# Two 1024-column projections by seven half-size products for eight, with their results kept in DRAM until they are used

## The chip, the cores and the metric

The kernel runs on one core of one Trainium2 chip. The metric is the time of one execution in microseconds of device time. Three runs of the kernel before gave 1104.89, 1106.11 and 1106.81 us.

## The reference

One decoder layer on 512 tokens of width 2048, in float32. Cut to what matters here:

```
h    = rmsnorm(x, norm_in)                       # 512 x 2048
proj = h @ w_in                                  # one projection, split by columns into
# q_a (1024), k_cmp v_cmp k_slc v_slc k_win v_win (256 each), gate_a (48), z_a (1024),
# q_h f_h i_h z_h (1024 each)
o_a  = nsa_mixer(q_a, k_cmp, ..., gate_a, ...)   # 16 query heads, 4 KV heads:
                                                 # compressed + selected + window attention
o_h  = hgrn2_mixer(q_h, f_h, i_h, lb)            # 8 heads, i_h is the values
o_a  = head_rmsnorm(o_a) * silu(z_a)
o_h  = head_rmsnorm(o_h) * silu(z_h)
x    = rmsnorm(x + concat(o_a, o_h) @ w_out)
```

In `compress_blocks`, blocks of 32 tokens of k_cmp (and v_cmp) go through two small matrices, `w1` and `w2`.

## The kernel before

Every large product of the kernel has a left factor and a right factor that are each split into a high part (rounded to the matmul's type) and a low part (the rest). Three matmuls make one product: high by high, low by high, high by low. `load_w` (L276 to L283) loads a tile of 128x1024 weights by one DMA of 512 KB on SP's queue, ACT casts it to the high part (L281), and DVE subtracts to get the low part (L282). The activations h stand transposed in SBUF as 16 tiles of 128 features by 512 tokens, high (`hh`) and low (`hl`), and stay there.

A projection comes in two forms. `proj_fm` (L323 to L325) puts features on the partitions: per 128 columns it takes 16 feature tiles times 3 = 48 matmuls of 128x512. `proj_tm` (L348 to L350) puts tokens on the partitions: for 512 columns it takes 16 feature tiles times 4 token tiles times 3 = 192 matmuls of 128x512. The program's order on PE, ACT and DVE is made by `run`, which takes turns between two streams of work in proportion to numbers written beside them. All DMAs but a few stand on SP's queue, in program order.

The stages are, in order: `first_proj` (k_cmp's columns, while x and the first weights arrive); the reciprocal norm of each token (`x_norm`: a chain of small DVE instructions that ends in L210 and L211, then transposes on PE, L214) ; `blocks`, which scales k_cmp (L367), copies it within SBUF into overlapping blocks by eight DMAs (L369 to L372, two tiles of four) and adds the position vectors (L383); v_cmp's projection alone; v_slc's projection beside the compression of k (`compress`, w1 loads at L390); v_win's projection with gate_a and then k_slc/k_win's first pairs (`make_kd(0, 0)`, `make_kd(0, 1)`) and q's first pair (`make_q(0)`), beside the compression of v; the attention with the other q and k projections between its steps; `hgrn_v(0)`, the first half of i_h, alone (192 matmuls); the eight heads of HGRN2, two at a time, each pair beside a length of other projections given by FILL = (62, 62.5, 62, 41): among them `hgrn_v(1)`, the second half of i_h, and both halves of z_a; the gates beside z_h; and the output projection. The attention's masks are made by GpSimd at the start.

Two results of `proj_tm` stay in SBUF: i_h as tiles of the pool `late` (13 buffers) and z_a as tiles of the pool `slab` (25 buffers).

Of the kernel before, what the change touches and what calls it, by code (L numbers as in the profile page):

```python
# [17 lines left out]
P = 128  # L18
# [14 lines left out]
NLATE = 13  # L33
PJ = 4
AHEAD = 2
FILL = (62, 62.5, 62, 41)
# [8 lines left out]
def hymba_layer(ctx: ExitStack, tc: tile.TileContext, x, norm_in, w_in, pe_k, w1_k, w2_k,  # L45
# [9 lines left out]
    slab = ctx.enter_context(tc.tile_pool(name="slab", bufs=NSLAB))  # L55
# [8 lines left out]

    def sl(dt=FP32):
        return slab.tile([P, 512], dt, name=nm("s"), tag="s")

    space = {}
# [7 lines left out]
    def b4(tag, bufs, dt=FP32):  # L76
        return big.tile([P, WCOLS], dt, name=nm(tag), tag=tag, bufs=bufs)
# [65 lines left out]
    def load_raw(src, k0, kt, c0, c, eng=None):  # L143
        raw = b4("w", WBUF)[:, 0:kt * c].rearrange("p (k c) -> p k c", k=kt)
        (eng or nc.sync).dma_start(out=raw, in_=src[k0 * P:(k0 + kt) * P, c0:c0 + c].rearrange("(k p) c -> p k c", p=P))
        return raw
# [4 lines left out]
    for k0, kt in FIRST:  # L151
        cs = slice(k0 * P, (k0 + kt) * P)
        first_w.append(load_raw(w_in2, k0, kt, C_KC, 256))
        if kt == 2:
            w = b4("w", WBUF).rearrange("p (t c) -> p t c", t=NT)
            nc.sync.dma_start(out=w, in_=x2[:, cs].rearrange("(t p) c -> p t c", p=P))
            xt.append([w[:, t, :] for t in range(NT)])
        else:
            xt.append([sl() for _ in range(NT)])
            for t in range(NT):  # L160
                nc.sync.dma_start(out=xt[-1][t], in_=x2[t * P:(t + 1) * P, cs])
# [58 lines left out]
    def consts():  # L220
# [28 lines left out]
    nc.gpsimd.affine_select(out=maskc, in_=maskc, pattern=[[P, NT], [-16, 32]], compare_op=ALU.is_ge,
                            fill=BIG, base=-31, channel_multiplier=1)  # L250
    keepc = const.tile([P, NT, 32], FP32, name="keepc")
    nc.gpsimd.memset(keepc, 1.0)
    nc.gpsimd.affine_select(out=keepc, in_=keepc, pattern=[[P, NT], [-16, 32]], compare_op=ALU.is_ge,
                            fill=0.0, base=-31, channel_multiplier=1)
    hmf = [sl(), sl()]
    hmask = const.tile([P, 8, 128], I32, name="hmask")
    for m in hmf:
        nc.gpsimd.memset(m, 1.0)

    def window(v, h, step, lo, width):  # L260
        nc.gpsimd.affine_select(out=v, in_=v, pattern=[[0, 2], [-step, P // step], [0, h]], compare_op=ALU.is_ge,
                                fill=0.0, base=-lo, channel_multiplier=1)
        nc.gpsimd.affine_select(out=v, in_=v, pattern=[[0, 2], [step, P // step], [0, h]], compare_op=ALU.is_ge,
                                fill=0.0, base=lo + width - 1, channel_multiplier=-1)


    for mi, (h, step, lo, width) in enumerate([(1, 2, 0, 1), (2, 4, 0, 2), (4, 8, 2, 2), (4, 8, 0, 2),
                                               (8, 16, 0, 8), (16, 32, 8, 8), (16, 32, 0, 8)]):
        v = hmf[mi // 4][:, (mi % 4) * P:(mi % 4 + 1) * P]
        window(v.rearrange("p (j b h) -> p j b h", j=2, h=h), h, step, lo, width)  # L270
    for i in range(2):
        nc.gpsimd.tensor_copy(hmask[:, 4 * i:4 * i + 4, :].rearrange("p a b -> p (a b)"), hmf[i])


    def load_w(src, k0, kt, c0, c, wt=None, raw=None):
        if raw is None:  # L276
            raw = load_raw(src, k0, kt, c0, c)
        if wt is None:
            wt = (b4("w", WBUF, F32R), b4("w", WBUF, F32R))
        hi, lo = [w[:, 0:kt * c].rearrange("p (k c) -> p k c", k=kt) for w in wt]  # L280
        nc.scalar.copy(hi, raw)  # L281
        nc.vector.tensor_tensor(lo, raw, hi.bitcast(FP32), ALU.subtract)  # L282
        return hi, lo  # L283

    def first_proj(acc):
# [3 lines left out]
        def prepare(c):  # L289
            w = load_w(w_in2, FIRST[c][0], FIRST[c][1], C_KC, 256, raw=first_w[c])  # L290
            x_turn(c)
            return w

        w = prepare(0)
        for c, (k0, kt) in enumerate(FIRST):
            hi, lo = w
            for j in range(2):
                js = slice(j * P, (j + 1) * P)
                for k in range(kt):
                    kk = k0 + k  # L300
# [739 lines left out]
```

## Time and profile before

| | us |
|---|---|
| median of three runs (range) | 1106.11 (1104.89 to 1106.81) |
| the profiled execution, whole | 1106.74 |
| its span in the trace | 1104.7 |
| PE busy in the span | 1086.3 |
| DVE busy | 572.0 |
| ACT busy | 394.3 |
| GpSimd busy | 76.1 |

The span is the time from the first to the last record of the core's engines and DMA queues. The granted TensorE clock had a mean of 0.997 of full speed over the span. Busy time of DVE, ACT and GpSimd lies beside PE's wherever the order of the program lets it.

### The profile page before, as it was taken

The numbers are of one execution on the slowest core, as the hardware profiler recorded it, in microseconds if no ns is written. First come the engines' busy times: TensorE is split into PE (matmuls) and PEld (weight loads), VectorE is DVE, ScalarE is ACT, GpSimd is POOL, SyncE is SP. The second block draws the span as 40 slices with busy tenths as digits, with TensorE's granted clock in tenths as the row PEclk, the third lists the DMA queues.
The fourth block names the chain that finished last, engine by engine and source line by source line (L and its number), as shares of the span: only waits on it lengthen the run. The fifth ranks groups of instructions, "written<-read, shape, count | busy, mean of one in ns | idle before, by whom it ended". The sixth has DMA issues, their size and how long they took to land.

```text
span 1104.7 us, 15078 instructions
## 1 busy us (share of the span) xinstructions
PE 1086.3 (98%) x5682; PEld 896.8 (81%) x5682; DVE 572.0 (52%) x1438; ACT 394.3 (36%) x798; POOL 76.1 (7%) x134
## 2 busy tenths in 40 slices
PE   7999999999999999999999999999999999999996
PEld 6899987777677777888888888888888888888886
DVE  4614336666655746416645547546677536324332
ACT  6412326645345644223222222223333423324221
POOL 5000020110200200000000000000000000202010
PEclk9999999999999999999999999999999999999998
DMA  7446454232422211323222322222242333335223
GB/s 256 122 142 191 115 145 104 71 83 58 115 59 57 76 39 39 96 77 96 77 77 61 92 78 80 82 81 73 76 130 81 95 115 115 126 112 173 96 86 124
DMA packets 91751, 109.60 MB, mean 99 GB/s; under 512 B 5584, under 2 KB 60448, under 8 KB 91680
## 3 DMA queue, kind: packets, MB, share of 16 engines
q1 hardware_dynamic: 91680, 108.65, 34.0%
q8 instruction: 45, 0.74, 0.3%
q14 instruction: 26, 0.21, 0.1%
HBM read 93.95 MB, written 4.19 MB: 89 GB/s over the span
## 4 chain that ended last, share of the span: by engine, by line
PE 94%; DMA 2%; ACT 1%; DVE 1%; issue 1%; SPq 0%; ACTq 0%
PE pj L348 13%; PE pj L349 13%; PE pj L350 13%; PE pj L323 10%; PE pj L325 10%; PE pj L324 10%; PE ot L581 4%; PE pj L562 3%; PE lp L730 3%; DMA w<-in_w_in_dram 2%; PE lp L548 2%; PE lp L549 1%; PE pj L973 1%; PE pj L972 1%; PE pj L974 1%; PE lp L399 1%
## 5 line engine op out<-in xcount | busy, mean ns | idle before, releaser
L282 DVE TENSOR_TENSOR w<-w,w 128x1024 fp32r<-128x1024 f32 (+3 forms) x151 | 182.3, 1208 | 255.7 <-PE pj L349 87.1
L281 ACT CAST w<-w 128x1024 fp32r<-128x1024 f32 (+3 forms) x151 | 156.8, 1039 | 300.1 <-DMA w<-in_w_in_dram 188.7
L348 PE MATMUL pj<-w,hh 128*128 128x512 f32 (+2 forms) x608 | 229.1, 377 | 0.0
L349 PE MATMUL pj<-w,hl 128*128 128x512 f32 (+2 forms) x608 | 225.1, 370 | 0.0
L350 PE MATMUL pj<-w,hh 128*128 128x512 f32 (+2 forms) x608 | 224.5, 370 | 0.0
L323 PE MATMUL pj<-hh,w 128*128 128x512 f32 x480 | 194.8, 406 | 0.0
L325 PE MATMUL pj<-hh,w 128*128 128x512 f32 x480 | 189.1, 394 | 0.0
L324 PE MATMUL pj<-hl,w 128*128 128x512 f32 x480 | 188.9, 393 | 0.0
L350 PEld LDWEIGHTS pj<-w,hh 128*128 128x128 f32 x608 | 114.2, 188 | 18.8
L348 PEld LDWEIGHTS pj<-w,hh 128*128 128x128 f32 x608 | 114.5, 188 | 18.1 <-ACT s L486 0.4
L349 PEld LDWEIGHTS pj<-w,hl 128*128 128x128 f32 x608 | 114.5, 188 | 17.7
L325 PEld LDWEIGHTS pj<-hh,w 128*128 128x128 f32 x480 | 90.2, 188 | 19.4 <-issue 0.9
L324 PEld LDWEIGHTS pj<-hl,w 128*128 128x128 f32 x480 | 90.4, 188 | 16.9 <-issue 0.5
L323 PEld LDWEIGHTS pj<-hh,w 128*128 128x128 f32 x480 | 90.3, 188 | 16.9 <-issue 0.7
L522 ACT ACTIVATE s<-s,mn 128x128 f32<-128x128 f32 (+3 forms) x128 | 71.7, 561 | 41.6 <-DVE mn L517 36.5
L517 DVE CUSTOM_DVE_ANT_0 s<-s,lp 128x128 f32<-128x128 f32 (+3 forms) x128 | 60.3, 483 | 37.2 <-PE lp L549 18.5
L562 PE MATMUL pj<-ident,s 128*128 128x128 f32 x320 | 53.7, 275 | 0.7 <-ACT s L522 0.5
L581 PE MATMUL ot<-pt,s 128*64 128x512 f32 (+3 forms) x256 | 47.9, 441 | 1.4 <-ACT pt L571 1.4
L562 PEld LDWEIGHTS pj<-ident,s 128*128 128x128 f32 x320 | 39.5, 140 | 11.1 <-ACT s L522 4.7
L571 ACT COPY pt<-pj 128x256 f32<-128x256 f32 (+2 forms) x56 | 25.8, 461 | 48.0 <-PE pj L562 47.8
L581 PEld LDWEIGHTS ot<-pt,s 128*64 128x64 f32 x256 | 22.2, 136 | 23.5 <-issue 10.5
L348 PE MATMUL pj<-w,s 128*128 128x512 f32 x96 | 37.5, 391 | 0.0
(252 smaller groups left out, 1350.8 us busy)
## 6 DMA issues: line engine op xcount, KB each, us to landing
w<-in_w_in_dram SPq DMA_DIRECT2D x115, 512.0 KB, 3.6
w<-in_w_out_dram SPq DMA_DIRECT2D x32, 512.0 KB, 3.8
s<-s SPq DMA_DIRECT2D x56, 128.0 KB, 2.3
s<-in_x_dram SPq DMA_DIRECT2D x16, 256.0 KB, 6.5
l<-in_x_dram SPq DMA_DIRECT2D x12, 256.0 KB, 3.2
out_dram<-l SPq DMA_DIRECT2D x12, 256.0 KB, 2.7
w<-in_w_in_dram SPq DMA_DIRECT2D x5, 456.0 KB, 4.6
w<-in_cmp_w_k_dram SPq DMA_DIRECT2D x4, 512.0 KB, 5.8
```

What stands on the lines that cost most here:

```text
L281: nc.scalar.copy(hi, raw)
L282: nc.vector.tensor_tensor(lo, raw, hi.bitcast(FP32), ALU.subtract)
L323: nc.tensor.matmul(acc[j], wh, hh, start=kk == 0, stop=False)
L324: nc.tensor.matmul(acc[j], wh, hl, start=False, stop=False)
L325: nc.tensor.matmul(acc[j], wl, hh, start=False, stop=kk == NK - 1)
L348: nc.tensor.matmul(o, ah, hi[:, k, :], start=kk == 0, stop=False)
L349: nc.tensor.matmul(o, al, hi[:, k, :], start=False, stop=False)
L350: nc.tensor.matmul(o, ah, lo[:, k, :], start=False, stop=kk == NK - 1)
L517: nc.vector.tensor_tensor_reduce(out=y, in0=e["bias"][:, 384 - i * P:512], in1=lp, scale=1.0, scalar=3e38, op0=ALU.add, op1=ALU.min, accum ...
L522: nc.scalar.activation(y, y, AF.Exp, bias=mn, scale=-1.0, accum_out=e["ls"][:, 2 * i + b:2 * i + b + 1])
L562: nc.tensor.transpose(tps[:, j * P:(j + 1) * P], y[:, j * P:(j + 1) * P], ident)
L581: nc.tensor.matmul(e["ot"][b * 64:(b + 1) * 64, j * P:512], v_tok[j][:, b * 256 + g * DH:b * 256 + (g + 1) * DH], e["pt"][:, b, j * 512:38 ...
```

## The change

- The four `proj_tm` of i_h and z_a (1024 columns each) are taken out of the places where they stood. In their place there are two calls of `seven`, one for i_h and one for z_a, one after the other, in a stage of their own ahead of the compression and the attention.
- `seven` multiplies 12 of the 16 feature tiles, in six pairs of tiles, by seven products of half the size in each direction in place of eight: the left halves are two halves of the tokens in two feature tiles of a pair, the right halves are two blocks of 512 columns. Seven times 36 = 252 matmuls of 128x512, and the last four feature tiles go as before, 96 matmuls: 348 for 1024 columns, where it was 384. Two calls make 696 for 768.
- For this the sums of the activations' quarters (S1 to S4, `sums_of`, six times) are made on DVE and split by ACT and DVE, beside the projections of v_cmp, v_slc and v_win. S3 is put over one quarter of h (`third_sums`), which goes to DRAM first and is read back (`block_21_back`) behind the seven products. The sums of the weights' blocks are made in `first`, `second` and `third` on DVE, and the products are added together by `after_first` to `after_all`, on DVE and ACT.
- Results go via DRAM: k_cmp and v_cmp (`keep`), v_slc and v_win (`vt_scr`), i_h (`v_scr`), z_a (`z_scr`). They are loaded again (`rows_back`, and `blocks`, whose eight DMAs now read DRAM) where they are used.
- The SBUF of the first part (pools `s2`, `s14`, `w` with 20 buffers, `e`) is given back (`first_part.close()`) before the slabs and the weight buffers of the rest are taken from it. The masks are made behind that, on GpSimd.
- The compression of k stands beside `make_kd(0, 0)` and `make_q(0)`, that of v beside `make_kd(0, 1)`. `late` has 18 buffers, FILL is (44, 42, 40, 24), and the gates of z_a's second half and of z_h's first half both stand beside the last projection.

The instructions on PE go from 5192 matmuls to 5120, no other change there in number. DVE gets 111 more instructions of 128x1024, 128x512 and 128x256, ACT 37 more of these sizes and 16 issues of DMAs, GpSimd 14 issues, and SP 38.

The diff, cut to its core:

```diff
-NLATE = 13
+NLATE = 18
-FILL = (62, 62.5, 62, 41)
+FILL = (44, 42, 40, 24)
+PAIRS = 6
...
+    def keep(acc):
+        fs = [dram(), dram()]
+        for j in range(2):
+            f = ev()
+            nc.vector.tensor_tensor(f, acc[j], rs_bc, ALU.mult)
+            nc.sync.dma_start(out=fs[j], in_=f)
+        return fs
     def blocks(acc, pcol):
         kv = []
         for j in range(2):
-            f = sl()
-            nc.vector.tensor_tensor(f, acc[j], rs_bc, ALU.mult)
+            f = acc[j]
             e, o = sl(), sl()
             nc.sync.dma_start(out=e[0:64, :], in_=f[0:64, :])
             nc.sync.dma_start(out=e[64:128, 0:511], in_=f[0:64, 1:512])
...
+        def first(jj):
+            b22, b12, b11 = load(1, jj, 1), load(0, jj, 1), load(0, jj, 0)
+            sub(b12, b12, b22)
+            t2[jj] = pair()
+            sub(t2[jj], b12, b11)
+            return parts(b11), parts(t2[jj]), parts(b12)
+        def second(jj):
+            b21, t4 = load(1, jj, 0), pair()
+            add(t4, t2[jj], b21)
+            return parts(t4), parts(b21)
...
+        return (group(first, (("A11", "1", True), ("S2", "6", True), ("S3", "7", True)), after_first) +
+                group(second, (("A22", "4", True), ("A12", "1", False)), lambda: None) + rest(0, "14", after_second) +
+                group(third, (("S1", "5", True), ("S4", "3", True)), after_third) + rest(1, "35", after_all))
...
-    kblk = blocks(KC, 32)
-    run((proj_fm(VC, C_VC, 256), 1))
-    run((proj_tm([], w_in2, hT, C_VS, 256, vs_done), 21), (compress(kblk, w1_k, w2_k, True), 10))
-    vblk = blocks(VC, 48)
-    run((chain(proj_tm([], w_in2, hT, C_VW, 304, vw_done), make_kd(0, 0), make_kd(0, 1), make_q(0)), 56),
-        (compress(vblk, w1_v, w2_v, False), 20))
+    kf = keep(KC)
+    run((chain(second_proj(VC), proj_tm([], w_in2, hT, C_VS, 256, vs_done), proj_tm([], w_in2, hT, C_VW, 304, vw_done)),
+         70), (all_sums(), 7))
+    third_sums()
+    in_turn(seven(C_IH, v_done) + seven(C_ZA, z_done(0)))
+    first_part.close()
...
+    block_21_back()
+    kblk = blocks(kf, 32)
+    masks()
...
+    run((chain(make_kd(0, 0), make_q(0)), 22), (compress(kblk, w1_k, w2_k, True), 10))
+    v_tok += rows_back(vt_scr, sl)
+    vblk = blocks(vf, 48)
+    run((chain(make_kd(0, 1)), 11), (compress(vblk, w1_v, w2_v, False), 10))
...
-    run((hgrn_v(0), 41))
+    hv[0] = rows_back(v_scr[0], late)
-    fill = chain(hgrn_qf(1), hgrn_v(1), hgrn_qf(2), hgrn_qf(3), z_proj(C_ZA, sz[0]), z_proj(C_ZA + 512, sz[1]))
+    fill = chain(hgrn_qf(1), hgrn_qf(2), hgrn_qf(3), z_proj(C_ZH, sz[2]))
...
-    run((fill, 41), (gate_chunk(0, o_nsa[0:4], 2, sz[0]), 10.5))
-    run((z_proj(C_ZH, sz[2]), 41), (gate_chunk(1, o_nsa[4:8], 2, sz[1]), 10.5))
-    run((z_proj(C_ZH + 512, sz[3]), 41), (gate_chunk(2, o_h[0:4], 1, sz[2]), 10.5))
+    sz[0] = rows_back(z_scr[0][0], sl)
+    run((fill, 15), (gate_chunk(0, o_nsa[0:4], 2, sz[0]), 10.5))
+    sz[1] = rows_back(z_scr[0][1], sl)
+    run((z_proj(C_ZH + 512, sz[3]), 41),
+        (chain(gate_chunk(1, o_nsa[4:8], 2, sz[1]), gate_chunk(2, o_h[0:4], 1, sz[2])), 21))
```

**First place: SP's queue ahead of `make_kd(0, 0)`.** In the kernel before, these are the loads of v_win's last weights and then of the first four tiles of `make_kd` (w<-in_w_in, 128x8x128):

```order
L145 DMA w_1150<-in_w_in_dram 128x3x304
L390 DMA w_1165<-in_cmp_w_v_dram 128x4x256
L145 DMA w_1202<-in_w_in_dram 128x3x304
L145 DMA w_1208<-in_w_in_dram 128x304
L145 DMA w_1304<-in_w_in_dram 128x8x128
L145 DMA w_1334<-in_w_in_dram 128x8x128
L145 DMA w_1383<-in_w_in_dram 128x8x128
L145 DMA w_1413<-in_w_in_dram 128x8x128
```

The loads of `make_kd` stood right behind other weights.

In the kernel after, SP's queue at the same load, with the last two weight tiles of `seven` (128x2x512) ahead of it; `d` is a tile in DRAM, `s` a slab:

```order
L160 DMA w_2213<-in_w_in_dram 128x2x512
L160 DMA w_2243<-in_w_in_dram 128x2x512
L607 DMA s_2362<-d_498 64x512
L608 DMA s_2362<-d_498 64x511
L609 DMA s_2363<-d_498 64x512
L610 DMA s_2363<-d_498 64x511
L607 DMA s_2368<-d_499 64x512
L608 DMA s_2368<-d_499 64x511
L609 DMA s_2369<-d_499 64x512
L610 DMA s_2369<-d_499 64x511
L160 DMA w_2440<-in_w_in_dram 128x8x128
L633 DMA s_2460<-in_cmp_w_k_dram 128x2x64 x2
```

Eight block loads of k_cmp now stand between the last weights of `seven` and the first weights of `make_kd(0, 0)`. The first of them (L607) writes a slab that lies where the first part's tiles lay, and its last wait is for PE: for the last matmul of `seven`. The next matmul on PE is the first of `make_kd(0, 0)`, with the weights of the L160 row.

**Second place: SP's queue ahead of the compression of v.** Before, its block loads stood between weights of v_win's projection:

```order
L145 DMA w_1098<-in_w_in_dram 128x3x304
L369 DMA s_948<-s_946 64x512
L370 DMA s_948<-s_946 64x511
L371 DMA s_949<-s_946 64x512
L372 DMA s_949<-s_946 64x511
L369 DMA s_956<-s_954 64x512
L370 DMA s_956<-s_954 64x511
L371 DMA s_957<-s_954 64x512
```

After, L687 are the copies of q's first pair, which wait for that projection's result, and L1072 the loads of v_slc's and v_win's results from DRAM:

```order
L160 DMA w_2758<-in_w_in_dram 128x8x128
L687 DMA s_2637<-s_2640 64x512
L687 DMA s_2637<-s_2641 64x512
L687 DMA s_2638<-s_2640 64x512
L687 DMA s_2638<-s_2641 64x512
L1072 DMA s_2649<-d_178 128x512
L1072 DMA s_2650<-d_179 128x512
L1072 DMA s_2651<-d_180 128x512
L1072 DMA s_2652<-d_181 128x512
L607 DMA s_2657<-d_672 64x512
L608 DMA s_2657<-d_672 64x511
L609 DMA s_2658<-d_672 64x512
```

The block loads of v_cmp moved behind four copies and four loads; behind `make_q(0)`, 48 matmuls of `make_kd(0, 1)` stand on PE, and then the first matmul of the compression of v, which needs these blocks.

**Third place: DVE in the chain of the reciprocal norm.** Before:

```order
L130 TENSOR_TENSOR rxt_481<-rxi_478 128x4
L131 TENSOR_TENSOR rxt_481<-rxt_481,rxa_476 128x4
L282 TENSOR_TENSOR w_547<-w_544,w_546 128x1024
L132 TENSOR_SCALAR rxt_481<-rxt_481 128x4
L133 TENSOR_TENSOR rxi_478<-rxi_478,rxt_481 128x4
L223 COPY col<-tp_462 128x64
L130 TENSOR_TENSOR rxt_481<-rxi_478 128x4
L226 TENSOR_TENSOR lbt<-col 128x8
L131 TENSOR_TENSOR rxt_481<-rxt_481,rxa_476 128x4
```

After, with the sums of the first two pairs (L362 adds the parts of h, L367 is one of the sums):

```order
L145 TENSOR_TENSOR rxt_477<-rxi_474 128x4
L146 TENSOR_TENSOR rxt_477<-rxt_477,rxa_472 128x4
L302 TENSOR_TENSOR w_511<-w_508,w_510 128x1024
L147 TENSOR_SCALAR rxt_477<-rxt_477 128x4
L362 TENSOR_TENSOR w_538<-hh_15_135,hl_16_136 128x1024
L242 COPY col<-tp_458 128x64
L148 TENSOR_TENSOR rxi_474<-rxi_474,rxt_477 128x4
L367 TENSOR_TENSOR w_538<-w_538 128x256
L245 TENSOR_TENSOR lbt<-col 128x8
```

A 128x1024 and a 128x256 instruction of the sums stand within the chain that PE's transposes and `keep` wait for.

## Rows read from the trace of the kernel before

**Rows 1.** The page: busy time of PE, and granted clock in 40 slices.

```profile
PE 1086.3 (98%) x5682; PEld 896.8 (81%) x5682; DVE 572.0 (52%) x1438; ACT 394.3 (36%) x798; POOL 76.1 (7%) x134
...
PEclk9999999999999999999999999999999999999998
```

**Rows 2.** Windows (us; busy of PE, PEld, DVE, ACT, POOL; clock, DMA share, GB/s).

```profile
0.00:25.00 25.00, 19.45 (x95) 16.26 (x96) 12.18 (x18) 16.11 (x37) 14.58 (x34) 1.00 0.84 275
...
475.00:500.00 25.00, 25.00 (x112) 20.72 (x111) 4.90 (x4) 6.87 (x8) 0.00 (x0) 1.00 0.30 82
```

**Rows 3.** Waits of PE: line, releaser, us in total, times, longest.

```profile
PE lp L192 <- DMA w<-in_x_dram: 3.0, 1, 3.0
...
PE ot L581 <- ACT pt L571: 1.4, 2, 0.8
...
PE tp L214 <- DVE rs L210: 0.2, 1, 0.2
```

**Rows 4.** Timeline of SP, the block copies (start, duration, line).

```profile
43.02 0.53 SPq L369 DMA_DIRECT2D s<-s  x1
43.60 0.58 SPq L370 DMA_DIRECT2D s<-s  x1
...
47.44 1.42 SPq L372 DMA_DIRECT2D s<-s  x1
```

**Rows 5.** DMA issues: KB each, median us to landing.

```profile
w<-in_w_in_dram SPq DMA_DIRECT2D x115, 512.0 KB, 3.6
...
s<-s SPq DMA_DIRECT2D x56, 128.0 KB, 2.3
```

**Rows 6.** The chain of waits that ended last: start, us, what.

```profile
254.31 4.21 DMA w<-in_w_in_dram
258.60 1.05 ACT w L281
```

**Rows 7.** Groups by line and shape: busy us, mean ns; idle before.

```profile
L282 DVE TENSOR_TENSOR w<-w,w 128x1024 fp32r<-128x1024 f32 x143 | 174.9, 1224 | 241.3 <-PE pj L349 85.7 <-ACT w L281 71.4 <-PE pj L324 54.7
...
L709 DVE TENSOR_TENSOR s<-s,s 128x256 f32<-128x256 f32 x56 | 23.9, 427 | 13.3 <-PE tp L775 9.3 <-POOL s L745 3.1 <-ACT s L759 0.2
...
L598 DVE TENSOR_TENSOR s<-tp,ls 128x512 f32<-128x512 f32 x16 | 11.0, 688 | 0.7 <-PE tp L596 0.4 <-ACT pt L571 0.3
...
L383 DVE TENSOR_TENSOR s<-s,col 128x124 f32<-128x124 f32 x32 | 9.2, 357 | 2.7 <-DMA s<-s 2.7
```

**Rows 8.** Timeline of PE at the start of the span.

```profile
5.81 1.12 PE L192 MATMUL lp<-ident,w 128*128 128x128 f32 x4 [3.04 <-DMA w<-in_x_dram]
...
9.51 0.63 PE L302 MATMUL pj<-hh,w 128*128 128x512 f32 x1
9.94 0.63 PE L303 MATMUL pj<-hl,w 128*128 128x512 f32 x1
...
12.68 0.40 PE L303 MATMUL pj<-hl,w 128*128 128x512 f32 x1
12.92 0.39 PE L304 MATMUL pj<-hh,w 128*128 128x512 f32 x1
```

**Rows 9.** Windows at the end of the span, behind PE's last work.

```profile
1096.00:1098.00 2.00, 0.00 (x0) 0.00 (x0) 1.56 (x9) 0.16 (x2) 0.00 (x0) 0.96 0.00 0
1098.00:1100.00 2.00, 0.00 (x0) 0.00 (x0) 1.30 (x3) 1.34 (x2) 0.00 (x0) 0.50 0.22 79
```

**Rows 10.** Timeline of DVE at the end of the norm's chain.

```profile
40.98 0.17 DVE L211 TENSOR_SCALAR rs<-rs 128x4 f32<-128x4 f32 x1
...
42.31 1.29 DVE L367 TENSOR_TENSOR s<-pj,rs_bc 128x512 f32<-128x512 f32 x2
```

**Rows 11.** Timeline of PE, the first matmul of v_cmp.

```profile
38.51 0.50 PE L323 MATMUL pj<-hh,w 128*128 128x512 f32 x1
```

**Rows 12.** Windows: a pair of HGRN2 heads, and the last pair.

```profile
582.50:666.70 84.20, 84.20 (x444) 70.53 (x443) 44.78 (x114) 25.15 (x47) 1.61 (x4) 1.00 0.28 78
...
748.30:808.00 59.70, 59.48 (x333) 49.68 (x332) 42.12 (x122) 18.74 (x40) 0.66 (x2) 1.00 0.30 89
```

More of the change, by code (lines that the diff above doesn't have):

```diff
@@ L63, in nm, with ev, dram @@
         return f"{s}_{cnt[0]}"
[L65 to L68 removed]
+    space, first_part = {}, ExitStack()
+    wbufs = [NU]
+    for name in ("s2", "s14", "w", "e"):
+        space[name] = first_part.enter_context(tc.tile_pool(name=name + "_first", bufs=1))
+    scr = ctx.enter_context(tc.tile_pool(name="scr", bufs=1, space=bass.MemoryType.DRAM))
+    def sl(dt=FP32):
+        return space["slab"].tile([P, 512], dt, name=nm("s"), tag="s", bufs=NSLAB)
+    def ev():
+        return space["e"].tile([P, 512], FP32, name=nm("e"), tag="e", bufs=NE)
+    def dram(shape=(P, 512)):
+        n = nm("d")
+        return scr.tile(list(shape), FP32, name=n, tag=n, bufs=1)
     def late():
@@ L267, in hymba_layer @@
[L267 to L280, printed above, removed]
+    cm = {}
@@ L281, in load_w, with parts @@
+    def parts(raw, to=None):
+        n, c = raw.shape[1], raw.shape[2]
+        hi, lo = [t[:, 0:n * c].rearrange("p (k c) -> p k c", k=n) for t in to or (b4(F32R), b4(F32R))]
         nc.scalar.copy(hi, raw)
@@ L308, in first_proj, with second_proj @@
                     x_squares(c)
+    def second_proj(acc):
+        acc += [pj(), pj()]
+        for k0 in range(0, NK, 4):
+            hi, lo = load_w(w_in2, k0, 4, C_VC, 256)
+            for j in range(2):
+                js = slice(j * P, (j + 1) * P)
+                for k in range(4):
+                    hh, hl = hT[0][k0 + k], hT[1][k0 + k]
+                    nc.tensor.matmul(acc[j], hi[:, k, js], hh, start=k0 + k == 0, stop=False)
+                    nc.tensor.matmul(acc[j], hi[:, k, js], hl, start=False, stop=False)
+                    nc.tensor.matmul(acc[j], lo[:, k, js], hh, start=False, stop=k0 + k == NK - 1)
+            yield 5.4
+        vf.extend(keep(acc))
@@ new lines, in all_sums, with third_sums, block_21_back @@
+    def all_sums():
+        for j in range(PAIRS):
+            sums_of(j)
+            yield 1.0
+    def third_sums():
+        for q in range(PAIRS // 2):
+            for part in range(2):
+                nc.gpsimd.dma_start(out=a21[part][q], in_=corner(q, part).bitcast(FP32))
+            hi, lo = [corner(q, part) for part in range(2)]
+            nc.scalar.copy(hi, s3[q])
+            nc.vector.tensor_tensor(lo, s3[q], hi.bitcast(FP32), ALU.subtract)
+    def block_21_back():
+        for q in range(PAIRS // 2):
+            for part in range(2):
+                nc.sync.dma_start(out=corner(q, part).bitcast(FP32), in_=a21[part][q])
@@ new lines, in in_turn, with v_done @@
+    def in_turn(steps):
+        ready = []
+        for n in range(len(steps) + AHEAD7):
+            if n < len(steps):
+                ready.append(steps[n][0]())
+            if n >= AHEAD7:
+                steps[n - AHEAD7][1](ready[n - AHEAD7])
+    v_scr = [[dram() for _ in range(NT)] for _ in range(2)]
+    z_scr = [[[dram() for _ in range(NT)] for _ in range(2)] for _ in range(2)]
+    vt_scr = [dram() for _ in range(NT)]
+    def v_done(half, t, src, y):
+        nc.scalar.mul(y, src, rs[:, 0, t:t + 1])
+        nc.scalar.dma_start(out=v_scr[half][t], in_=y)
@@ L310, in proj_fm, with z_done, done @@
+    def z_done(which):
+        def done(half, t, src, y):
+            th = ev()
+            nc.scalar.activation(th, src, AF.Tanh, scale=rs[:, 1, t:t + 1])
+            nc.vector.scalar_tensor_tensor(y, th, 1.0, src, ALU.add, ALU.mult)
+            nc.gpsimd.dma_start(out=z_scr[which][half][t], in_=y)
+        return done
     def proj_fm(acc, c0, c):
@@ L463, in make_kd @@
         else:
-            t = [small.tile([P, 672], F32R, name=nm("kw"), tag="kw", bufs=KWB) for _ in range(4)]
+            t = [space["att"].tile([P, 672], F32R, name=nm("kw"), tag="kw", bufs=KWB) for _ in range(4)]
             v = [a[:, 160:672] for a in t]
@@ L826, in hymba_layer, with rows_back @@
     hq, hf_, hv = {}, {}, {}
-    def hgrn_v(c):
-        hv[c] = [late() for _ in range(NT)]
-        def done(t, acc):
-            nc.scalar.mul(hv[c][t], acc, rs[:, 0, t:t + 1])
-        yield from proj_tm([], w_in2, hT, C_IH + c * 512, 512, done)
+    def rows_back(scr_, alloc):
+        tiles = [alloc() for _ in range(NT)]
+        for t in range(NT):
+            nc.sync.dma_start(out=tiles[t], in_=scr_[t])
+        return tiles
     def hgrn_qf(c):
```

245 lines of the change are left out of this document (193 added, 52 removed).

## The prediction

> **What bounds the kernel now.** I read the busy times first, then windows along the span, then the waits of PE. PE is busy 1086.3 of 1104.7 us, at full clock in all slices but the last [rows 1]. In a stretch of plain projections it has no gap at all: 25.00 of 25.00 us with 112 matmuls of 128x512, so 25.00 / 112 = 0.2232 us each [rows 2]. Its waits are short: the longest is the first arrival of x (3.0 us), and inside the program the largest is 1.4 us in sum [rows 3]. So the kernel is a queue of matmuls. Two things follow. A matmul taken off is worth its full 0.223 us, wherever it stood. And a wait put before a matmul is lost in full, because nothing behind it on PE has slack. The profiled execution took 1106.74 us, span 1104.7 and 2.0 around it; the median of the runs is 0.6 us lower, and I sum against the profiled one and take 0.4 off at the end for where the median lies.
>
> **Matmuls removed.** Two calls of `seven` at 348 in place of 384: 72 matmuls of 128x512, 72 x 0.2232 = **-16.1 us**. The whole gain is this; the quarter sums and casts are on DVE and ACT.
>
> **The seam behind the seven products.** Before, the first weights of `make_kd(0, 0)` were loaded while PE worked on v_win. Now SP's queue reaches the eight block loads of k_cmp first, and the first of these waits for the last matmul of `seven`, since it writes into space that the first part held. The weights of PE's very next matmul stand behind these eight. So from the end of that last matmul PE has nothing to do until this chain is through:
> - the signal from PE to SP, about 0.1 us;
> - eight issues: in the same eight copies before, the first starts at 43.02 and the last at 47.44, so 4.42 / 7 = 0.63 each, 8 x 0.63 = 5.05 us [rows 4];
> - the weights' load from issue to landing: 3.6 us in the median [rows 5], 4.2 where the chain of waits ran through one [rows 6]; the queue holds the eight block loads too, so I take 3.9;
> - ACT's cast, 1.05 us [rows 6].
> That is 10.1 us for the first matmul. The third matmul of a product needs the low part, a 1.22 us subtraction on DVE [rows 7]; two matmuls cover 0.45 to 0.85 of it, so 0.5 more. The 16 additions of the position vectors (L383 in the kernel before) stand ahead of it on DVE: their blocks land by 5.05 + 2.3 = 7.4 us [rows 5], and at 0.36 each [rows 7], most of them before the last landing, they are done by about 9, ahead of the cast. So **10.6 us** of idle, between 9.5 (issues of 0.53, the shorter load, no wait for the low part) and 12 (a load held up by the eight ahead of it by a landing's half, 1.2 us).
>
> Then the clock. At the start of the span, PE begins to work at 5.81 with matmuls 0.43 us apart, and by 12.68 they are 0.24 us apart [rows 8]. At the end, PE has no work from 1096 on; the granted clock is 0.96 in 1096:1098 and 0.50, the lower level of 1.2 GHz, from 1098 on [rows 9]. There the clock fell after a few idle us, so 10.6 us of idle should be enough. Restarting at half pace costs half of the slow stretch: (12.68 - 5.81) / 2 = 3.4 us by the start, nothing if the level came back at once; I take **3**, as it is the nearest case. Nothing on the other engines is late then, since they work ahead. The seam costs 10.6 + 3 = **13.6 us** (9.5 to 15.4).
>
> The Trainium skill, TensorE: Matmul & The Clock Gate, Part 1 (The HAM clock gate), says that "the default state is throttled, and activity releases the throttle". By that rule the restart at the seam must be paid once more, as at the start; if the clock were a thing of the program's start alone, the sum would be 3 us less. The trace agrees with the rule at both of its ends, the start and the 0.50 behind PE's last work; a gap of this length inside the program, the trace doesn't show.
>
> **The compression of v.** Its first matmul stands 48 matmuls, 48 x 0.2232 = 10.7 us, behind `make_q(0)`. Its blocks' loads stand in SP's queue behind four copies of q's first pair (which wait for its scaling, cast and subtraction, some 2 us at 0.69 for a 128x512 pass [rows 7]) and four loads of v: 16 issues x 0.6 = 9.6 us after that [rows 4], landing 2.3 us later [rows 5], the last additions, about 0.4. The blocks are there at 2 + 9.6 + 2.3 + 0.4 = 14.3 at most, 13 if the first copies go earlier. PE waits **3 us** (0 to 4). Here the gap is short and the clock half stays; I take nothing for it.
>
> **The norm's chain and v_cmp.** A 128x1024 and a 128x256 sum now stand inside the chain before L211: 1.22 + 0.43 us [rows 7]. The scaling of k_cmp and its two stores come that much later, v_cmp's third weight tile stands behind these stores on SP, and two tiles of weights cover only 48 matmuls = 10.7 us from 38.5 [rows 11]. Before, the chain ended at 41.0 and the scaling ran at 42.3 to 43.6 [rows 10]; now the first store is at about 45, the load issued at 45.8, landed 49.4, cast by 50.5, against 49.2: **1 us** (-0.2, PE's old wait for this chain [rows 3], to 3).
>
> **Inside the seven products.** A step of `first` is 36 matmuls = 8.0 us and needs five DVE passes of 1.22 = 6.1 us, 3.2 of ACT, and 1.5 MB: at the 275 GB/s of the first 25 us [rows 2] 5.7 us. All fit. `second` and `third` need 3 x 1.22 = 3.7 in 5.4 us. The hand-over between groups puts four additions of 0.69 before the next low part: 0.3 to 0.7 us. I take **0.7** (0 to 3). The sums of the activations lie beside v_cmp, v_slc and v_win, over 80 us of PE, some 24 us of DVE: nothing. The masks' 14.6 us of GpSimd in the first 25 [rows 2] move behind the seam and are needed only in the attention: nothing.
>
> **Heads and gates.** The work of the heads on DVE stays, the cover on PE shrinks from 62 to 40 or 44 a pair. In the second pair PE had 84.2 and DVE 44.8 us; in the last, 59.5 and 42.1 [rows 12]. A fill of 41 is 192 matmuls, 42.9 us, so the second pair keeps 84.2 - 20.5 x 1.045 = 62.8 us on PE, and the last one, with 24 for 41, 59.5 - 17.8 = 41.7 us. There DVE loses the low parts of 17/41 of eight weight tiles, 4 us, and has 38 of 41.7 us. It is tight only there, and the work before it can run ahead. The gates lie two in one projection. I take **1 us** (0 to 4). Loading v, z back costs SP's issues only, far ahead of use.
>
> **Sum.** -16.1 + 13.6 + 3 + 1 + 0.7 + 1 = **+3.2**; 1106.7 + 3.2 = 1109.9, less 0.4 = **1109.5 us**. The low ends of all terms would give 1106.3 - 16.1 + 9.5 = 1099.7, the high ends 1106.3 - 16.1 + 15.4 + 4 + 3 + 3 + 4 = 1119.6.
>
> **Rivals.**
> - *The clock holds over the seam, or comes back at once.* Then the 3 us fall away: 1106.5. For it: the fall at the end of the span came behind a stretch of small matmuls, not of dense ones. Against it: 0.50 within a few us of PE's last work [rows 9].
> - *The seam is short, so the kernel is faster.* If SP isn't held until the last matmul (the slabs' space free earlier, or the first weights put where nothing is waited for), the eight issues and most of the load go under the last products: of 10.6 us only 0 to 3 stay, and no clock is lost: 1106.3 - 16.1 + 2 + 5.7 = 1098. It decides from the point where the block loads start over 7 us before the last product's end, since then the gap is too short for the clock. Midway (3 us of gap saved and no clock lost) is 1103. Against it: SP's first block load waits on that very matmul.
> - *DVE becomes the bound in the last heads and gates.* From the point where DVE's 38 us with its waits for PE and ACT fill PE's 41.7, each us more is lost: 6 us there in place of 1: 1114.5. For it: DVE's idle in a head is in many short waits for PE [rows 7]. Against it: PE had no gaps with DVE at 71% [rows 12].
> - *The change doesn't do what it says in the seven products*: DVE and ACT wait on each other, and a step of `first` takes 9 us for 8: 6 steps, plus hand-overs, 6 to 8 us more: 1116.
>
> **How the numbers follow.** Forecast (1107 to 1113) 0.48; clock holds 0.16; short seam 0.20; heads bound 0.11; seven products bound 0.05. A measurement of this kernel can tell about 0.2%, 2.2 us, from no change. Slower than 1108.3: 0.41 of the forecast's, the last two, 0.02 of the clock's: 0.58. Within: 0.07 + 0.12 + a little: 0.20. Faster than 1103.9: the short seam's and 0.02: 0.22. The range of 8 in 10 runs from 1100 to 1115; it leaves out half of the short seam and the worst of the last two. The likeliest case's own range is 1107 to 1113.
>
> **What would show it.** Right: one gap on PE of 9.5 to 12 us between the last L465 and the first L555, ended by ACT's cast, with a granted clock of 0.5 for some us behind it; a second one of about 3 us at the compression of v; 72 matmuls fewer at 0.223. Wrong: a gap of under 7 us at the seam (then the short seam), PE gaps of several us in the last heads with DVE full, or gaps spread through the seven products.

## The result: slower by 3.8%, and the profile after

The changed kernel took 1147.88 us in the median (1146.91 to 1149.26, four runs), the kernel before 1106.46 us beside it. The ratio is 1.038 (95% interval 1.036 to 1.040): 41 us slower, where 3 us slower was forecast and 1115 us was the upper end of the range.

The page of the profiled execution (span, busy time of the engines, busy tenths of PE and granted clock in 40 slices) answers [rows 1]:

```profile
span 1145.2 us, 15222 instructions
...
PE 1096.8 (96%) x5610; PEld 887.3 (77%) x5610; DVE 657.8 (57%) x1549; ACT 420.3 (37%) x835; POOL 85.7 (7%) x148
...
PE   7999999989598999999999999999999999999996
...
PEclk9999999989798999999999999999999999999998
```

PE has 72 instructions less and yet is busy 10.5 us longer, and the two rows of tenths dip together in slices 9, 11 and 13, between some 230 and 370 us into the span. The waits of PE, which answer [rows 3]:

```profile
PE pj L555 <- ACT w L301: 12.3, 1, 12.3
PE lp L637 <- issue: 5.1, 1, 5.1
...
PE lp L453 <- ACT w L301: 3.7, 1, 3.7
...
PE pj L453 <- ACT w L301: 1.6, 2, 1.4
PE tp L453 <- ACT w L301: 1.5, 2, 1.3
PE pj L342 <- ACT w L301: 1.2, 1, 1.2
```

In the changed kernel, L453 to L455 are the products of `seven`, L555 to L557 are `proj_fm`, L637 the compression and L342 v_cmp. The 12.3 us are the seam behind the seven products, the 5.1 us the compression of v, the 1.2 us v_cmp: the three waits that the prediction named. The waits at L453 it did not have. These make 25 us. But the time went up by 41 us although 16 us of matmuls went away, so 57 us were lost, and 32 of them are not waits of PE. Two views of windows (start and end, us; busy time of PE, PEld, DVE, ACT, POOL; granted clock) show part of it:

```profile
113.80:287.20 173.40, 166.05 (x697) 131.91 (x696) 100.46 (x102) 60.87 (x69) 2.71 (x5) 0.98 0.39 126
...
234.00:238.00 4.00, 4.00 (x11) 3.10 (x10) 2.83 (x3) 1.86 (x2) 0.00 (x0) 0.50 0.44 131
...
300.00:306.00 6.00, 5.81 (x16) 4.14 (x15) 2.06 (x2) 1.05 (x1) 3.67 (x7) 0.50 1.03 285
...
349.40:354.00 4.60, 4.55 (x21) 4.58 (x22) 2.06 (x4) 1.71 (x2) 4.36 (x7) 0.50 0.73 179
```

The first is the whole stretch of the two calls of `seven`: 173.4 us for 696 matmuls, 15.6 more than 696 x 0.2267. The others are the moments behind the waits of 3.7, 12.3 and 5.1 us: each time PE restarts at a granted clock of 0.50, 1.2 GHz. And what is left is in the matmuls' own steps. In the output projection, the same code as before, the timeline of PE (start, duration, line) has one step where the stationary side is `hh` and another where it is `s`:

```profile
1070.22 0.40 PE L581 MATMUL pj<-w,hl 128*128 128x512 f32 x1
1070.46 0.39 PE L582 MATMUL pj<-w,hh 128*128 128x512 f32 x1
1070.69 0.40 PE L580 MATMUL pj<-w,hh 128*128 128x512 f32 x1
1070.93 0.40 PE L581 MATMUL pj<-w,hl 128*128 128x512 f32 x1
...
1052.02 0.39 PE L582 MATMUL pj<-w,s 128*128 128x512 f32 x1
1052.24 0.39 PE L580 MATMUL pj<-w,s 128*128 128x512 f32 x1
1052.47 0.39 PE L581 MATMUL pj<-w,s 128*128 128x512 f32 x1
1052.70 0.39 PE L582 MATMUL pj<-w,s 128*128 128x512 f32 x1
```

With `hh` and `hl` the starts are 0.237 us apart in the mean of these (0.71 in three) and 0.234 over all matmuls of this kind in the trace, with `s` 0.227 (0.68 in three), at full clock and with no wait. Before, the same line stepped by 0.227 with `hh` too:

```profile
1029.76 0.39 PE L348 MATMUL pj<-w,hh 128*128 128x512 f32 x1
1029.99 0.39 PE L349 MATMUL pj<-w,hl 128*128 128x512 f32 x1
1030.22 0.39 PE L350 MATMUL pj<-w,hh 128*128 128x512 f32 x1
```

### The profile page after: what moved, and what is told of

It reads as the page before. It is cut to its first block, busy times and chain, and to the rows that moved or that the text cites. A ratio compares the mean times of both kernels' runs of the same rounds, so it can differ in the third digit from the quotient of the medians.

```text
span 1145.2 us, 15222 instructions
## 1 busy us (share of the span) xinstructions
PE 1096.8 (96%) x5610; PEld 887.3 (77%) x5610; DVE 657.8 (57%) x1549; ACT 420.3 (37%) x835; POOL 85.7 (7%) x148
## 4 chain that ended last, share of the span: by engine, by line
PE 84%; DVE 5%; DMA 4%; issue 4%; ACT 2%; SPq 1%; POOL 0%; ACTq 0%; DVEq 0%; POOLq 0%
PE pj L580 8%; PE pj L581 8%; PE pj L582 8%; PE pj L557 8%; PE pj L555 8%; PE pj L556 8%; DMA w<-in_w_in_dram 4%; PE ot L822 4%; PE pj L803 3%; PE lp L971 2%; PE pj L453 2%; PE pj L455 2%; PE pj L454 2%; PE lp L637 1%; PE lp L789 1%
## 5 line engine op out<-in xcount | busy, mean ns | idle before, releaser
L302 DVE TENSOR_TENSOR w<-w,w 128x1024 fp32r<-128x1024 f32 (+3 forms) x169 | 203.1, 1214 | 163.7 <-ACT w L301 67.3
L301 ACT CAST w<-w 128x1024 fp32r<-128x1024 f32 (+3 forms) x169 | 172.3, 1036 | 252.0 <-DMA w<-in_w_in_dram 151.7
L555 PE MATMUL pj<-hh,w 128*128 128x512 f32 x448 | 186.2, 416 | 12.3 <-ACT w L301 12.3
L557 PE MATMUL pj<-hh,w 128*128 128x512 f32 x448 | 179.1, 400 | 0.2 <-DVE w L302 0.2
L580 PE MATMUL pj<-w,hh 128*128 128x512 f32 (+2 forms) x352 | 127.9, 364 | 0.0
L581 PE MATMUL pj<-w,hl 128*128 128x512 f32 (+2 forms) x352 | 126.8, 361 | 0.0
L582 PE MATMUL pj<-w,hh 128*128 128x512 f32 (+2 forms) x352 | 126.6, 360 | 0.0
L555 PEld LDWEIGHTS pj<-hh,w 128*128 128x128 f32 x448 | 84.9, 189 | 29.9 <-ACT w L301 12.7
L557 PEld LDWEIGHTS pj<-hh,w 128*128 128x128 f32 x448 | 84.7, 189 | 20.9 <-issue 1.0
L582 PEld LDWEIGHTS pj<-w,hh 128*128 128x128 f32 x352 | 66.2, 188 | 9.6
L580 PEld LDWEIGHTS pj<-w,hh 128*128 128x128 f32 x352 | 66.3, 189 | 9.3
L581 PEld LDWEIGHTS pj<-w,hl 128*128 128x128 f32 x352 | 66.3, 189 | 9.1
L822 PE MATMUL ot<-pt,s 128*64 128x256 f32 (+3 forms) x256 | 46.6, 441 | 0.7 <-ACT pt L812 0.4
L971 PE MATMUL lp<-s,s 128*128 128x192 f32 x192 | 35.9, 330 | 2.0 <-ACT s L1000 1.8
```

The lines of the kernel that those rows point to most:

```text
L555: nc.tensor.matmul(acc[j], wh, hh, start=kk == 0, stop=False)
L557: nc.tensor.matmul(acc[j], wl, hh, start=False, stop=kk == NK - 1)
L580: nc.tensor.matmul(o, ah, hi[:, k, :], start=kk == 0, stop=False)
L581: nc.tensor.matmul(o, al, hi[:, k, :], start=False, stop=False)
L582: nc.tensor.matmul(o, ah, lo[:, k, :], start=False, stop=kk == NK - 1)
L822: nc.tensor.matmul(e["ot"][b * 64:(b + 1) * 64, j * P:512], v_tok[j][:, b * 256 + g * DH:b * 256 + (g + 1) * DH], e["pt"][:, b, j * 512:38 ...
```

## Experiments

Each is one edit of the changed kernel unless it says otherwise; the time is the median, beside runs of the kernel before on the same chip (1105.65 to 1106.51 us). Edits that add lines shift the line numbers: `proj_fm` is L555 or L558, the compression L637, L640 or L662.

### e1: the same remainder for both operands

What the program's SBUF addresses tell: in the kernel before, h and the weight tiles lie in one pool, and both start at multiples of 64 bytes. In the changed kernel the weights have pools of their own behind the pool of small tiles, which holds 1952 bytes, and 1952 is 32 more than a multiple of 64: h starts at a multiple of 64, weights, slabs and the sums S1, S2 and S4 at 32 beyond one. A matmul reads one tile as its moving and one as its stationary side. Of the 3400 matmuls of 128x512 in the trace, 2832 have h (`hh` or `hl`) as one side and so different remainders; of the 568 others, 504 have both sides in the new pools, as in the `w,s` rows above.

```diff
-    big = ctx.enter_context(tc.tile_pool(name="big", bufs=1))
     small = ctx.enter_context(tc.tile_pool(name="small", bufs=2))
+    big = ctx.enter_context(tc.tile_pool(name="big", bufs=1))
```

> The changed kernel with one edit: the pool of small tiles is taken from SBUF ahead of the pool that holds h. This moves h by 1952 bytes, so that h and the weight tiles start at the same remainder of 64 bytes (32 and 32), where it was 0 and 32; no instruction is added, removed or moved. Theory A (a 128x512 matmul whose two operands in SBUF start at different remainders of 64 takes about 233.5 ns in place of 227): 2832 matmuls of the changed kernel are of that kind, at 6 to 7 ns each 17 to 20 us go away, so 1128 to 1131 us from 1147.9, and in the trace the output projection steps by 0.227 us. Theory B (the slower pace comes from the added traffic of DMAs and DVE, or from the granted clock): 1146 to 1150. Theory C (each operand that doesn't start at a multiple of 64 costs by itself): h is off too now, so no gain or a loss, 1147 to 1155.

Measured: 1134.43 us (1131.39 to 1140.42), 13.5 us less. In the timeline of PE the output projection steps by 0.227:

```profile
1069.69 0.39 PE L580 MATMUL pj<-w,hh 128*128 128x512 f32 x1
1069.92 0.39 PE L581 MATMUL pj<-w,hl 128*128 128x512 f32 x1
1070.15 0.39 PE L582 MATMUL pj<-w,hh 128*128 128x512 f32 x1
```

So B falls: the traffic is the same, and three of the four runs had a mean granted clock of 0.981 to 0.986, no higher than the changed kernel's 0.984 to 0.986 (the fourth, the profiled one with 1131.39 us, had 0.992). C falls too: both sides now start at 32 beyond a multiple of 64, and the step is that of two multiples of 64. Theory A overestimated the size by a quarter; e9 returns to it.

### e2: the kernel before, with different remainders

```diff
-    slab = ctx.enter_context(tc.tile_pool(name="slab", bufs=NSLAB))
     small = ctx.enter_context(tc.tile_pool(name="small", bufs=2))
+    wpool = ctx.enter_context(tc.tile_pool(name="wpool", bufs=1))
+    slab = ctx.enter_context(tc.tile_pool(name="slab", bufs=NSLAB))
...
-        return big.tile([P, WCOLS], dt, name=nm(tag), tag=tag, bufs=bufs)
+        return wpool.tile([P, WCOLS], dt, name=nm(tag), tag=tag, bufs=bufs)
```

> The kernel before with one edit: the weight tiles get a pool of their own behind the pool of small tiles, and the slabs follow it, so that weights and slabs start at 32 beyond a multiple of 64 bytes and h at a multiple of 64, as in the changed kernel; no instruction is added, removed or moved. Theory A (different remainders of the two operands cost 6 to 7 ns a matmul): some 3400 matmuls of 128x512 become of that kind, a fifth of them slower already beside the attention, so 16 to 23 us more: 1122 to 1130. Theory B (added traffic or the clock): 1104 to 1109.

Measured: 1122.16 us (1121.56 to 1122.47), ratio 1.0145 (1.013 to 1.016): 16 us more, with not one instruction changed. PE's timeline of its output projection has both steps again, 0.24 with `hh` and 0.227 with `s`:

```profile
1010.38 0.40 PE L351 MATMUL pj<-w,hh 128*128 128x512 f32 x1
1010.62 0.40 PE L349 MATMUL pj<-w,hh 128*128 128x512 f32 x1
1010.86 0.40 PE L350 MATMUL pj<-w,hl 128*128 128x512 f32 x1
...
1030.24 0.39 PE L350 MATMUL pj<-w,s 128*128 128x512 f32 x1
1030.47 0.39 PE L351 MATMUL pj<-w,s 128*128 128x512 f32 x1
```

This is 5.1 ns for each of the 3120 matmuls of 128x512 in its trace that have h as one side. With e1 this settles where the pace comes from: where the two sides lie against each other. Only one distance was tried, 1952 bytes, which leaves 32 by 128 as well as by 64, so that 64 is the number that counts is not shown.

### e3: reading h's quarter back on another queue

```diff
-                nc.sync.dma_start(out=corner(q, part).bitcast(FP32), in_=a21[part][q])
+                nc.gpsimd.dma_start(out=corner(q, part).bitcast(FP32), in_=a21[part][q])
```

> The changed kernel with the six DMAs that read the saved quarter of h back moved from SP's queue to GpSimd's; nothing else changes. Theory A (each pair of these waits on SP for the last use of that quarter, and the weight loads of the second call of seven queue behind it): PE's gaps of 1.3 and 3.7 us near 213 and 229 go, and the half clock behind the second (about 2.7 us): 5 to 8 us less, 1140 to 1143. Theory B (the gaps come from DVE's passes over the weights, which then have as little time as before): within 2 us of 1147.9.

Measured: 1136.74 us (1134.59 to 1137.42), 11.1 us less, more than expected. In the changed kernel, SP's timeline shows what stood where (L398 reads back, L416 loads weights), and the chain of waits what came of it:

```profile
204.33 0.64 SPq L398 DMA_DIRECT2D hl<-d  x1
205.07 0.54 SPq L398 DMA_DIRECT2D hh<-d  x1
205.71 1.58 SPq L416 DMA_DIRECT2D w<-in_w_in_dram  x3
...
223.07 0.52 SPq L398 DMA_DIRECT2D hl<-d  x1
223.70 0.55 SPq L398 DMA_DIRECT2D hh<-d  x1
224.35 1.06 SPq L416 DMA_DIRECT2D w<-in_w_in_dram  x2
```

```profile
224.35 5.85 DMA w<-in_w_in_dram
...
230.22 1.23 DVE w L408
...
232.58 0.79 PE lp L453
```

The code writes `block_21_back` behind the seven products, but its DMAs stand in SP's queue between weight loads of the second call, each waiting for the last use of S3 in that quarter of h. The weights behind it came 5.85 us after 224.35, and PE stood from 228.9 to 232.6. With the six DMAs on GpSimd's queue the gaps at 213 and 229 are gone, with the half clock behind the second, and the stretch of `seven` takes 165.0 us for 173.4:

```profile
112.60:277.60 165.00, 162.85 (x698) 130.33 (x696) 100.33 (x102) 60.87 (x69) 7.02 (x11) 1.00 0.42 133
```

That is 8.4 of the 11.1 us. Most of the rest: the wait for the compression of v was 2.5 us in place of 5.1.

### e4: the first weights ahead of the block loads

```diff
     block_21_back()
+    kd0 = make_kd(0, 0)
+    first_kd = [next(kd0) for _ in range(4)]
     kblk = blocks(kf, 32)
...
-    run((chain(make_kd(0, 0), make_q(0)), 22), (compress(kblk, w1_k, w2_k, True), 10))
+    run((chain(kd0, make_q(0)), 22), (compress(kblk, w1_k, w2_k, True), 10))
```

> The changed kernel with one edit: the first four steps of the k_slc projection (its two weight loads among them) are written ahead of the block loads of k_cmp; SP's queue then has the first weights ahead of the eight block loads and the second behind four of them. Theory A (the weights stood behind the eight block loads, which wait for the last matmul of seven): PE's gap of 12.3 us shrinks to 0 to 3 and the half clock of 3.4 us behind it goes: 12 to 15 us less, 1133 to 1136. Theory B (the weights' own buffers are free only at the end of seven, whatever the queue): the issues alone are saved, 5 us less, and the clock still falls: 1142 to 1144.

Measured: 1142.61 us (1140.46 to 1143.91), 5.3 us less: theory B. SP's timeline at the seam (the last matmul of `seven` ends at 287.7):

```profile
287.74 0.37 SPq L160 DMA_DIRECT2D w<-in_w_in_dram  x1
288.16 0.59 SPq L607 DMA_DIRECT2D s<-d  x1
...
290.75 0.59 SPq L160 DMA_DIRECT2D w<-in_w_in_dram  x1
```

The first weight load now stands ahead of all block loads and still starts only at the last matmul's end, although its buffer lies where S2 lay, whose last use was some 240 matmuls earlier. By the program's waits, the first tile that is taken from space given back waits for the last user of all of it. PE's gap is 5.3 us there, and the compression of v, which now has fewer matmuls right ahead of it, waits 9.0 us for its blocks in place of 5.1. So my account of the seam was half right: the queue was in the way, but behind it the buffer was.

### e5: weights in space that stays

The weights of the first part rotate through two pools of ten buffers; one of them is kept for the rest of the program, so that k_slc's first weights wait for single buffers. The edit of e4 is in it.

```diff
-    for name in ("s2", "s14", "w", "e"):
+    space["w"] = ctx.enter_context(tc.tile_pool(name="w", bufs=1))
+    for name in ("s2", "s14", "wx", "e"):
...
+        wbufs[0] += 1
+        pool = space["wx"] if "wx" in space and wbufs[0] % 2 else space["w"]
...
     first_part.close()
+    del space["wx"]
```

> The changed kernel, with the first four steps of the k_slc projection written ahead of the block loads as in e4, and with weights that rotate through two pools of ten buffers: one of them is not given back behind seven, so the first weights of k_slc need wait only for their own buffer. Theory A (what held the weights in e4 was the giving back of all the first part's space at once, which waits for the last matmul of seven): PE's gap of 12.3 us behind seven goes to 0 to 1 us, with its half clock of 3.4, and the compression of k, 60 matmuls on, finds its blocks nearly there: 12 to 16 us less than 1147.9, 1132 to 1136. Theory B (the wait only moves to the compression, which waits for the block loads as it did 9.0 us in e4): 5 to 9 us less, 1139 to 1143.

Measured: 1118.79 us (1117.23 to 1120.20), 29.1 us less; both theories had less. PE's waits and the stretch of `seven`:

```profile
PE lp L640 <- DVE s L624: 7.0, 1, 7.0
...
111.40:272.90 161.50, 161.50 (x698) 130.91 (x697) 99.46 (x98) 60.73 (x68) 2.73 (x5) 1.00 0.48 148
```

The seam has no gap any more. `seven` has none either: with the other rotation of buffers the six DMAs that read back stand behind more of the weight loads, so this edit also did what e3 did. Taken against e3, the gain is 1136.7 - 1118.8 = 18 us, and 14.4 between the two profiled runs. It isn't the seam's alone: the stretch of `seven` takes 161.5 us for 165.0, so 3.5 us of it lie there; the seam's gap, 11.9 us in e3, is gone with the half clock behind it; and the compression of v, now 7.0 us with a half clock behind it, takes back 4.5.

### e6 and e7: the edits together, and the blocks of v_cmp earlier

e6 has the edits of e1, e3 and e5.

> The edits of e1 (both operands at the same remainder of 64), e3 (reading back on GpSimd's queue) and e5 (weights in space that stays) together. If the three losses are separate they add: 1147.9 - 13.5 - 11.2 - 14 = 1109, 1105 to 1113. If a faster PE meets the next wait (DVE's passes in seven, the block loads), a third or more of the sum is lost: 1114 to 1122.

Measured: 1106.86 us (1106.15 to 1107.63), ratio 1.0005 (0.9996 to 1.0015): level with the kernel before. Over e5 it is 11.9 us, the remainder's share; reading back on GpSimd's queue gives nothing more. PE waits 6.3 us at the compression of v.

e7 also has

```diff
-    v_tok += rows_back(vt_scr, sl)
     vblk = blocks(vf, 48)
+    v_tok += rows_back(vt_scr, sl)
```

> As e6, with the block loads of v_cmp written ahead of the four loads of v's tokens on SP's queue. Theory A (the compression of v waits for its blocks behind those four issues): 2 to 5 us less than e6. Theory B (it waits for the copies of q's first pair, or for something else): within 1.5 us of e6.

Measured: 1099.66 us (1099.11 to 1100.93), 7.2 us less than e6 and more than theory A had, ratio 0.9942 (0.9926 to 0.9957): faster than both kernels, by 0.6% against the kernel before. Four issues moved, 2.0 us in SP's timeline, took 4.2 us off the wait, and the half clock behind it went too. From the first matmul behind `seven` to the first of the attention, e7 takes 61.4 us for 67.0 in e6; the rest of the 7.2 us lies elsewhere in the span, and no run shows why. The wait in e6, then the wait, the stretch of `seven` and the window behind the wait in e7:

```profile
PE lp L640 <- DVE s L624: 6.3, 1, 6.3
```

```profile
PE lp L640 <- DVE s L624: 2.1, 1, 2.1
...
112.70:270.50 157.80, 157.80 (x699) 130.64 (x698) 99.37 (x98) 60.56 (x68) 7.04 (x11) 1.00 0.50 152
...
314.70:320.00 5.30, 5.30 (x48) 5.30 (x49) 0.46 (x2) 0.13 (x1) 4.07 (x8) 1.00 1.08 296
```

The stretch of `seven` is now 157.8 us, 696 x 0.2267: its five DVE passes a step and its hand-overs cost nothing.

### e8: plain products in the same place

e7 with both calls of `seven` replaced by plain products, 192 matmuls for each 512 columns, and nothing read back.

```diff
-    third_sums()
-    in_turn(seven(C_IH, v_done) + seven(C_ZA, z_done(0)))
+    in_turn(eight(C_IH, v_done) + eight(C_ZA, z_done(0)))
...
-    block_21_back()
```

> e7 with the two calls of seven taken back to plain products (768 matmuls of 128x512 in place of 696, four token tiles by sixteen feature tiles for each 512 columns), in the same place, with results via DRAM as in e7; the sums of the activations are still made, but S3 isn't put over h and nothing is read back. Theory A (the saving of the seven products is 72 matmuls at 0.2267 us and nothing of it is lost any more in e7): 16.3 us more than e7's 1099.7, 1114.5 to 1117.5. Theory B (the extra passes of DVE and ACT, or the hand-overs between the groups, eat a part in e7): 8 to 13 us more, 1108 to 1113.

Measured: 1119.73 us (1117.12 to 1120.79), 20.1 us more than e7, above both theories. In the profiled runs, 20.5 us apart, the stage of the products takes 174.1 us for 157.8, so 16.3 of it are the 72 matmuls. From there to the attention's first matmul it is 63.4 us for 61.4: the wait for the compression of v, 2.7 us for 2.1, was followed this time by a restart at half clock. Another 3.1 us are lost between there and the last part of the output projection, and no run shows why.

```profile
PE lp L662 <- DVE s L646: 2.7, 1, 2.7
...
329.00:335.00 6.00, 5.64 (x26) 5.67 (x27) 0.91 (x4) 0.85 (x1) 3.90 (x8) 0.50 1.12 307
```

So the seven products are worth their full 72 matmuls in their stage, and what goes around them (the stage of its own, results via DRAM) costs e8 some 14 us against the kernel before.

### e9: e7 with different remainders

e7 without the edit of e1.

> e7 without the edit of e1: h starts again at a multiple of 64 bytes and the weights 32 beyond, so 2832 matmuls of 128x512 have operands at different remainders, as in the changed kernel. Theory A (each of them costs 6 to 7 ns, and in e1 a part of the 17 to 20 us was lost again because a faster PE met waits that are gone here): 17 to 20 us more than e7's 1099.7, 1116.5 to 1119.5. Theory B (the size is what e1 showed, about 13.5 us, 4.8 ns a matmul): 1112 to 1114.

Measured: 1111.92 us (1110.57 to 1112.97), 12.3 us more: theory B on the size. From the starts in PE's timelines, the mean step between 128x512 matmuls that follow each other and have h as one side is 234.1 ns here and 226.7 in e7 over `seven`, 233.5 and 230.0 over the attention, 233.5 and 228.8 over the heads, 234.1 and 227.5 behind them. So the 7 ns hold where projections stand alone; beside other work the steps with equal remainders are partly longer already, and there the difference is 3 to 5 ns. End to end it is 12.3 us, 4.3 ns over all 2832, for 4.8 in e1 and 5.1 in e2.

A wait of PE in the same place, the compression of v, was followed by a half clock here and not in e7: 2.0 us here (316.5 to 318.4), 2.1 there.

```profile
319.60:323.00 3.40, 3.40 (x18) 3.40 (x17) 0.00 (x0) 0.00 (x0) 3.07 (x7) 0.50 1.12 315
```

And in e1 PE waited 2.8 and 3.2 us within `seven`, and the granted clock stayed at full behind both; the window right behind the second, in which PE is at work again:

```profile
231.80:240.00 8.20, 8.16 (x35) 6.60 (x36) 7.01 (x7) 4.85 (x5) 0.00 (x0) 1.00 0.49 138
```

So in these runs the length of a wait of 2 to 3 us doesn't tell whether a half clock follows it.

## Why the prediction was wrong

Where the 41 us come from, by the runs (the lines overlap a little and add up to 42):

| | us | from |
|---|---|---|
| 72 matmuls fewer | -16.3 | 72 x 0.2267; the stage in e8 against e7 |
| operands at different remainders of 64 | +12 to 14 | e1, e9 |
| reading back in SP's queue, with its half clock and 2.6 at the compression of v | +11 | e3 |
| the seam, with its half clock, and 3.5 more within `seven` | +18 | e5 against e3 (14.4 between the profiled runs) |
| blocks of v behind the loads of v's tokens, with its half clock | +7 | e7 against e6 |
| left in e7 | +9.5 | 1099.7 against 1106.5 - 16.3 |

- **The matmuls removed: right.** The unit was a little off: the window's count of 112 takes in matmuls that only touch its edges. The starts are 0.2267 apart, so 16.3 and not 16.1 us.
- **A matmul's price taken as fixed: this step failed first, and cost 12 to 14 us.** "72 x 0.2232" and every count of matmuls after it held the step of a matmul constant; the sum had no term for 2832 others that got slower. It could not be read from a view of the trace of before, where both sides always had the same remainder. It could have been seen in the program: the change moves the weights and slabs into other pools, so all addresses change.
- **Inside the seven products: the term failed, 0.7 forecast (0 to 3), 11.9 measured** (173.4 us for the 161.5 of e5, with the same remainders): 6.9 of gaps over 0.4 us, some 2.7 by the half clock (an estimate, half of the 5.4 us from PE's restart at 232.6 to the end of the half clock at 238.0), and 2.3 that lie in neither. The step weighed the rates of DVE, ACT and DMA, and these did fit, as e7 shows. It left out the order in SP's queue, where six DMAs with waits for PE stand among the weight loads. I had looked at SP's order at the seam and the compression, and not there. "Gaps spread through the seven products" stood in the prediction as a sign of being wrong, and it came.
- **The seam: right in kind and in the clock, small in size, half right in its cause.** 10.6 + 3 forecast; the gap was 12.3 us, just beyond the 9.5 to 12 that were to show it, and that low end of 9.5 adds up to 9.0 from its own terms (0.1 + 8 x 0.53 + 3.6 + 1.05). The weights stood behind the block loads, but without these they still waited for their buffer (e4). In the chain the eight issues took 5.2 us, as forecast from [rows 4], and the load behind them 5.84 us where 3.9 were taken:

```profile
287.20 0.49 SPq L607
...
291.79 0.61 SPq L610
...
292.44 5.84 DMA w<-in_w_in_dram
```

  The load's price came from the median of [rows 5], a load among few others; here it ran with eight more in flight. The restart at half clock was there, 0.50 in 300:306. The Trainium skill's rule (TensorE: Matmul & The Clock Gate, Part 1) that activity releases a throttle which is the default agrees with it, and with the two further restarts that I hadn't counted.
- **The compression of v: the place right, the size not.** 3 forecast, 5.1 measured, and "the clock half stays" was wrong: 0.50 in 349.4:354.
- **v_cmp: right**, 1.2 us for 1.
- **Heads and gates: somewhat small.** From the attention's first matmul to the first of the output projection's last part (L972 before, L1237 in e7), before took 883.7 us and e7 711.6, with 768 matmuls or 174.1 us taken out of the stretch: 2 us more, for 1 forecast (0 to 4). In e1, e6 and e8, where the remainders are equal too, the stretch took 713.8, 715.0 and 714.7 us: 4 to 5 us more.
- **The rivals.** The short seam was given 0.20 and would have needed more than the order of a queue, as e4 shows. The rival of the seven products, given 0.05, had a loss of that size there, 6 to 8 us, but put it to DVE and ACT. The case that came, several things at once that none of the terms held, had no chance of its own, and 1119.6, the sum of all high ends, was below the measured time.

Not settled: of the 9.5 us left in e7, 7 are lost ahead of the attention (PE's first matmul of it comes at 331.9 in e7; 167.1 before plus the 157.8 of `seven` would be 324.9), and its waits there, 2.1, 1.2 and 0.9 us and 0.8 at the first loads, make 5 of them.

## What to carry to other kernels

A change that moves tiles to other pools changes addresses, and addresses are part of a matmul's price: look at where both sides of a matmul start before counting matmuls. A queue must be read row by row over the whole stretch that a change touches, since a DMA with a wait written behind a loop can land inside it. And space that is given back in one piece makes its first new user wait for its last old one, so the weights that come next belong in space that stays.

## What the runs showed of the hardware

A 128x512 float32 matmul stepped by 0.227 us when its moving and stationary tiles began at the same remainder of 64 bytes, both 0 or both 32, and by 0.234 in the mean when one was 0 and the other 32. Moving them apart cost the kernel before 16 us (1.45%), with no other difference. Other remainders weren't tried. The granted clock fell to 0.50 behind idle times of PE of 2.0 (e9), 2.5 (e3), 2.7 (e8), 3.7, 5.1 and 12.3 us, and stayed at 1.00 behind 2.1 us in e7 and behind 2.8 and 3.2 us in e1.
